# Keys and values of an encoder layer's input projection by pairs of k tiles, seven block products for 14 of 32 pairs

## The chip, the cores and the metric

The kernel runs on one core of one Trainium2 chip, in one launch. The metric is the device time in microseconds, as the median of several runs. Engines are named as in the profile: PE (matmuls; PEld is its weight load), DVE (the vector engine), ACT (the scalar engine), POOL (GpSimd) and SP, which only issues DMAs.

## What is computed

One encoder layer on 256 tokens with 2048 features, all in float32: a layer norm, an input projection to six groups of 1024 columns, two kinds of attention, an output projection, and a gated feed-forward network. Cut to what matters here:

```python
h = layer_norm(x, ln_in_g, ln_in_b)                      # x: (256, 2048)
proj = h @ w_in                                          # (2048, 6144)
na_q, na_k, na_v, d_q, d_k, d_v = split(proj, 6)         # 1024 columns each
na_out = neighbourhood_attention(na_q, na_k, na_v, na_rpb)          # 8 heads of 128
diff_out = rms_norm(differential_attention(d_q, d_k, d_v, lam, rel_bias_table), diff_subln_g)  # 4 heads
h = layer_norm(ALPHA * h + concat(na_out, diff_out) @ w_out, ln1_g, ln1_b)
h = layer_norm(ALPHA * h + (silu(h @ w_gate) * (h @ w_up)) @ w_down, ln2_g, ln2_b)
```

## The kernel before

**Matmuls.** Every float32 operand is cut into a rounded high part and the remainder, and a product is three matmuls: high by high, high by low, low by high. A *unit* is one k tile (128 rows) of one group's weights, 1024 columns wide. The six groups of the input projection are worked off in the order dq, dk, dv, nq, nk, nv, 16 units each; then come w_out (o0 and o1), the gate and up projections (f, g and u groups) and w_down. There are two token tiles, t = 0 and 1. In the input projection before the change, `mm_step` multiplies one unit by one token tile: six matmuls of 128x512, so 24 for a pair of units and both token tiles. The first eight units of dq (`NF0`) are multiplied for t = 0 in plain float32, unsplit, since nothing has been split yet ("whole" steps, two slow matmuls each).

**Pairs.** The gate, up and down projections already take their units in pairs (`add_group(..., seven)`). A pair is a 2x2 block matrix on each side. Plain pairs take eight block products; pairs named in `SEVEN` take seven (Winograd's form of Strassen's scheme). One block product is three matmuls. Seven products need sums of weight blocks and sums of token blocks ("forms", made by `more_forms`), each of which is split into high and low parts again. `seven_parts` lists this work for the weights of a pair: eleven operations on ACT and DVE in place of four. At the end of a group, `ffn_ends` combines the products on DVE into four blocks and hands each to `block_end`.

**Who sets the order.** The program is one stream per engine, written by a planner in the kernel: it keeps a clock for each engine, walks the list of PE steps (`steps`), and between them emits weight splits (`next_part`) up to `AHEAD_S` = 24 steps ahead and side work (attention heads, transposes, forms: `Side`), as its own clocks find it due. Engines then run their streams in order and wait for each other by semaphores. All SBUF tiles of 4 KB a partition come from one pool of 46 slots; a weight load needs a free slot, and SP issues loads in order.

**Names in rows.** `sl` is a slot, `acc` a PSUM bank, `nb`, `s` and `o` are small rings; `hT` is the transposed, split, normalised input; `h` are the normalised rows in their natural layout, which the residual sum of w_out needs again. Nearly every instruction is recorded at one helper line (L53, after the change L54), so groups are told apart by tiles and shapes.

Of the kernel before, what the change touches and what calls it, by code (L numbers as in the profile page):

```python
# [252 lines left out]
def layer_kernel(ctx: ExitStack, tc: tile.TileContext, A: dict, out: bass.AP):  # L253
# [61 lines left out]
    def chunk(ts, c):  # L315
        return ts[c // 2][:, (c % 2) * 512 : (c % 2) * 512 + 512]
# [47 lines left out]

    h_d = dram.tile([2 * P, D], F32, name="h_d")
    mid_d = dram.tile([NFC * P, 1024], F32, name="mid_d")
# [54 lines left out]
    def mm_step(t, u):  # L421
# [14 lines left out]
        if t == 1:  # L436
            leave(hi, lo)
            g, k = un["group"], un["k"]
            if k % 4 == 3:
                if g == "nv":  # L440
                    leave(*hT_tiles[k // 4])
                elif g == ("o", 1):
                    leave(*mixT_tiles[k // 4])
# [18 lines left out]
    L2 = 8  # L462
    R0 = 3
    R1 = 8
# [61 lines left out]
    def ln_side(key, t, g, b, store, tiles, n_whole):  # L526
# [10 lines left out]
        for c in range(4):  # L537
            while (key, t, c, "norm") not in have:
                yield None
            if t == 1 and c % 2:  # L540
                leave(g[c // 2], b[c // 2])
            yield "pe", [chunk(h[t], c)]
            if c not in tiles:
                new_T(store, tiles, c)
            bk = pe_transpose4(chunk(h[t], c))
            if key == "1":
                nc.gpsimd.dma_start(h_d[t * P : (t + 1) * P, c * 512 : (c + 1) * 512], chunk(h[t], c))
                if c % 2:
                    leave(h[t][c // 2])
                if c not in hF:  # L550
                    hF[c] = slot([P, 4, S])
                f = hF[c][:, :, t * P : (t + 1) * P]
                nc.scalar.copy(f, bk.rearrange("p (a b) -> p a b", b=P))
                have["hF", c] = have.get(("hF", c), 0) + 1
                if t == 0 and 4 * c < n_whole:
                    for i in range(4):
                        whole[key][4 * c + i] = f[:, i, :]
                    have[key, "whole", c] = 1
                side.add(part_split(key, t, c, f, tiles[c], t == 0 and 4 * c < n_whole))
                if t == 1:  # L560
                    for i in range(2):
                        side.add(more_forms(2 * c + i))
            elif t == 0 and 4 * c < n_whole:
                f = ring("nb", 2, (P, 4, P))
                nc.scalar.copy(f, bk.rearrange("p (a b) -> p a b", b=P))
# [3 lines left out]
                side.add(whole_split(key, c, f, tiles[c]))  # L569
            else:  # L570
                evac_T(bk, *tiles[c], t)
                have[key, t, c] = 1

    def whole_split(key, c, f, parts):
        return part_split(key, 0, c, f, parts, True)

    def part_split(key, t, c, f, parts, late):
# [7 lines left out]
        have[key, t, c] = 1  # L585
        if key == "1":
            used(("hF", c), 4, hF[c])

    hF, forms, halves, form_slots = {}, {}, [], []

    def more_forms(i):
        c, k = i // 2, 2 * (i % 2)
        while have.get(("hF", c), 0) < 2:
            yield None
        yield "dve", [hF[c]]
        ab, cd = hF[c][:, k : k + 2, :P], hF[c][:, k : k + 2, P:]
        if i in SEVEN:  # L600
            n = 4
            f = ring("s", 4, (P, 4, P))
# [534 lines left out]
    def products(u):  # L1137
# [7 lines left out]
        def f(m):  # L1145
            return lambda: forms[u if is_down(u) else i][m]

# [47 lines left out]
    def take_product(u, n):  # L1195
# [11 lines left out]
        if over:  # L1207
# [3 lines left out]
            if u == SE - 2:  # L1211
                leave(*[x for c in range(4) for x in h1T_tiles[c]], *form_slots)
            if is_down(u):
# [85 lines left out]

    ln1 = {}  # L1300

    ln2 = {}

# [6 lines left out]
    def group_out(t, name, a):  # L1310
        if name in ("dq", "dk", "nq", "nk"):
# [3 lines left out]
            nc.vector.tensor_scalar(nat[:, 512:], a[1], sc, None, op0=ALU.mult)  # L1315
            side.add(qk_side(name, t, nat), first=True)
            if t == 1 and name == "dk":
                for hd in range(DF_H):
                    side.add(diff_head(hd))
            if t == 1 and name == "nq":  # L1320
                for hd in range(NA_H):
                    side.add(na_head(hd))
        elif name in ("dv", "nv"):
# [71 lines left out]
    def steps():  # L1395
# [74 lines left out]
    class Step:  # L1470
# [18 lines left out]
        def possible(self):  # L1489
            if self.kind == "product":  # L1490
                k = units[self.u]["k"]
                if is_down(self.u):
# [122 lines left out]
```

## Time and profile before

| | us |
|---|---|
| median of 3 runs (1127.6 to 1128.8) | 1128.45 |
| the profiled execution's own time | 1128.12 |
| its span, first to last instruction | 1126.0 |
| PE busy in the span | 1110.7 |
| DVE busy | 929.1 |
| ACT busy | 596.9 |

The profiled execution is 2.1 us longer than its span and 0.3 us below the median of the runs. PE is busy nearly throughout, and the granted clock is 0.998 of full speed. The input projection runs from about 29 us to about 320 us of the span, the last attention heads until about 333 us; DVE is busy two thirds of that stretch and nearly all of the feed-forward network.

### The profile page before, as it was taken

What the parts mean: (1) busy time and instruction counts of PE and PEld (TensorE: products, weight loads), DVE (VectorE), ACT (ScalarE), POOL (GpSimd) and SP (SyncE); (2) the same over time, 40 slices, a digit from 0 to 9 for tenths busy, and PEclk for the clock granted to TensorE, in tenths of its full rate; (3) what the DMA queues carried; (4) which work ended last, traced back from release to release, by engine and by line L of the source; (5) the groups of instructions that cost most, each with busy time, mean ns of one, the idle gap of its engine ahead of it and who ended that gap; (6) DMA issues with size and microseconds to landing.
All of it is one profiled execution on the core that took longest, in us unless ns stands there. A gap on an engine that the chain in (4) does not pass through costs nothing.

```text
span 1126.0 us, 14140 instructions
## 1 busy us (share of the span) xinstructions
PE 1110.7 (99%) x5028; PEld 903.8 (80%) x5028; DVE 929.1 (83%) x1263; ACT 596.9 (53%) x781; POOL 59.6 (5%) x111
## 2 busy tenths in 40 slices
PE   8999999999999999999999999999999999999997
PEld 4788888888788876888888888888888888878885
DVE  7863876547773669999999999999999999799865
ACT  5552556434563228656556556566566566545630
POOL 2000003110100020000000000000000000000001
PEclk9999999999999999999999999999999999999999
DMA  9764548795766754655754755855756877667752
GB/s 332 246 204 156 166 146 172 177 206 187 162 218 231 243 183 135 210 197 173 268 206 164 278 205 164 282 190 178 271 208 223 289 265 281 217 223 281 251 164 75
DMA packets 70407, 237.15 MB, mean 211 GB/s; under 512 B 8516, under 2 KB 9924, under 8 KB 70336
## 3 DMA queue, kind: packets, MB, share of 16 engines
q1 hardware_dynamic: 65008, 220.49, 57.7%
q0 software_dynamic: 5168, 15.68, 6.8%
q8 instruction: 39, 0.64, 0.2%
q14 instruction: 32, 0.26, 0.1%
q10 hardware_dynamic: 160, 0.08, 0.0%
HBM read 226.25 MB, written 9.97 MB: 210 GB/s over the span
## 4 chain that ended last, share of the span: by engine, by line
PE 49%; issue 41%; DVE 5%; POOL 2%; ACT 2%; DMA 1%; POOLq 0%; DVEq 0%; ACTq 0%
PE acc L53 49%; DVE sl L53 3%; POOL mid_d L53 1%; ACT s L53 1%; DVE stats L53 1%; DVE s L53 1%; DMA mid_d<-nb 1%; ACT sl L53 1%; POOL rstd L53 0%; DMA nb<-in_ln_in_b_dram 0%; POOL h_d L53 0%; POOL rs L53 0%; ACT o L53 0%; DVE o L53 0%; ACT nb L53 0%
## 5 line engine op out<-in xcount | busy, mean ns | idle before, releaser
L53 PE MATMUL acc<-sl,sl 128*128 128x512 f32 (+1 forms) x4676 | 1062.8, 388 | 2.3 <-DVE sl L53 1.4
L53 PEld LDWEIGHTS acc<-sl,sl 128*128 128x128 f32 x4676 | 860.6, 188 | 183.7 <-issue 6.2
L53 DVE TENSOR_TENSOR sl<-sl,sl 128x1024 fp32r<-128x1024 f32 (+3 forms) x710 | 682.7, 1015 | 44.0 <-ACT sl L53 35.4
L53 ACT ACTIVATE sl<-sl 128x1024 fp32r<-128x1024 f32 (+1 forms) x530 | 498.6, 994 | 272.3 <-DVE sl L53 138.4
L53 ACT ACTIVATE sl<-acc 128x256 fp32r<-128x256 f32 (+2 forms) x70 | 33.2, 498 | 92.5 <-PE acc L53 74.0
L53 DVE TENSOR_TENSOR sl<-acc,sl 128x256 fp32r<-128x256 f32 (+2 forms) x94 | 54.8, 596 | 28.4 <-ACT sl L53 21.6
L53 DVE TENSOR_TENSOR sl<-sl 128x512 f32<-128x512 f32 (+1 forms) x76 | 41.2, 556 | 0.0
L53 DVE SCALAR_TENSOR_TENSOR sl<-sl,acc 128x512 f32<-128x512 f32 x10 | 6.8, 677 | 36.6 <-PE acc L53 36.6
L53 POOL DMA_DIRECT2D mid_d<-nb x22 | 11.9, 542 | 458.6 <-ACT nb L53 458.6
L53 ACT COPY sl<-acc 128x512 f32<-128x512 f32 x30 | 16.5, 587 | 34.9 <-PE acc L53 34.9
L53 DVE TENSOR_SCALAR sl<-acc 128x512 f32<-128x512 f32 x8 | 5.5, 688 | 34.2 <-PE acc L53 34.2
L53 ACT COPY nb<-acc 128x512 f32<-128x512 f32 x24 | 14.0, 585 | 34.9 <-PE acc L53 30.4
L53 ACT ACTIVATE s<-s 128x512 f32<-128x512 f32 x20 | 12.3, 632 | 22.8 <-DVE s L53 22.8
L53 POOL DMA_DIRECT2D nb<-in_na_rpb_dram x32 | 19.7, 624 | 85.7 <-DVE s L53 85.7
L53 ACT ACTIVATE s<-s,mx 128x256 f32<-128x256 f32 x32 | 15.9, 499 | 15.4 <-DVE mx L53 15.4
L53 PE MATMUL acc<-ident,s 128*128 128x128 f32 x136 | 20.5, 274 | 2.3 <-DVE s L53 1.7
L53 PEld LDWEIGHTS acc<-ident,s 128*128 128x128 f32 x136 | 16.5, 140 | 7.3 <-issue 1.9
L53 PEld LDWEIGHTS acc<-ident,sl 128*128 128x128 f32 x128 | 15.0, 140 | 7.3 <-issue 3.5
L53 DVE TENSOR_TENSOR sl<-sl,acc 128x512 f32<-128x512 f32 x16 | 10.6, 680 | 12.3 <-PE acc L53 12.2
L53 DVE SCALAR_TENSOR_TENSOR sl<-sl,rstd,sl 128x512 f32<-128x512 f32 x22 | 16.5, 752 | 4.0 <-POOL rstd L53 3.1
L53 DVE BATCH_NORM_STATS2 stats<-sl 128x6 f32<-128x512 f32 x24 | 16.3, 691 | 3.0 <-DMA sl<-in_x_dram 2.4
L53 PE MATMUL acc<-ident,sl 128*128 128x128 f32 x128 | 17.6, 273 | 0.5 <-DVE sl L53 0.4
(78 smaller groups left out, 224.4 us busy)
## 6 DMA issues: line engine op xcount, KB each, us to landing
sl<-in_w_in_dram SPq DMA_DIRECT2D x96, 512.0 KB, 4.8
sl<-in_w_down_dram SPq DMA_DIRECT2D x88, 512.0 KB, 6.0
sl<-in_w_gate_dram SPq DMA_DIRECT2D x80, 512.0 KB, 4.4
sl<-in_w_up_dram SPq DMA_DIRECT2D x80, 512.0 KB, 4.5
sl<-in_w_out_dram SPq DMA_DIRECT2D x32, 512.0 KB, 5.0
sl<-mid_d SPq DMA_DIRECT2D x14, 512.0 KB, 4.0
mid_d<-nb POOLq DMA_DIRECT2D x22, 256.0 KB, 3.3
sl<-in_w_gate_dram SPq DMA_DIRECT2D x16, 256.0 KB, 4.4
```

What stands on the lines that cost most here:

```text
L53: result = getattr(self.engine, op)(*args, **kw)
```

## The change

The groups dk, dv, nk and nv are now taken by pairs too. `SEVEN_IN` names the pairs with seven products: pairs 0, 2, 4 and 6 of dk and nk, pairs 0, 2 and 4 of dv and nv, 14 of 32 in all; the other 18 take eight products. dq and nq stay as they were.

- The normalised input now goes the way that the rows ahead of the feed-forward network went already: each chunk of transposed rows is copied to a slot (`hF`), split from there, and the forms are made from it, now under keys ("in" or "1"). Pair 6 needs both kinds of forms for "in".
- After its transposes each chunk of normalised rows is written to DRAM by POOL (`h_in`, eight DMAs of 256 KB), its slots are given back, and four loads of 512 KB on SP bring the rows back at unit 10 of o0.
- `R0` falls from 3 to 1: the second token tile of dq catches up with the first by the end of dq, because a pair needs both.
- The four groups end in `block_end`, which adds the products into a natural tile on DVE; keys are then transposed and values split (`v_side`) from there.
- Plain forms use ring `o` in place of half of ring `s`, in the feed-forward network too.

```diff
+SEVEN_IN = dict(dk=(0, 2, 4, 6), dv=(0, 2, 4), nk=(0, 2, 4, 6), nv=(0, 2, 4))
...
-        add_group(name, range(KT), [W_IN[:, off : off + 1024]], hT)
+        add_group(name, range(KT), [W_IN[:, off : off + 1024]], hT, SEVEN_IN.get(name))
...
-        if un["group"] == ("d", 0) and un["k"] == 24:
+        if (un["group"], un["k"]) in ((("o", 0), 10), (("d", 0), 24)):
+            key = "in" if un["group"][0] == "o" else "1"
             for t in range(2):
                 h[t] = [slot([P, 1024]) for _ in range(2)]
                 for i in range(2):
-                    nc.sync.dma_start(h[t][i], h_d[t * P : (t + 1) * P, i * 1024 : (i + 1) * 1024])
+                    nc.sync.dma_start(h[t][i], h_d[key][t * P : (t + 1) * P, i * 1024 : (i + 1) * 1024])
...
-    R0 = 3
+    R0 = 1
...
+            nc.gpsimd.dma_start(h_d[key][t * P : (t + 1) * P, c * 512 : (c + 1) * 512], chunk(h[t], c))
+            if c % 2:
+                leave(h[t][c // 2])
+            if (key, c) not in hF:
+                hF[key, c] = slot([P, 4, S])
+            f = hF[key, c][:, :, t * P : (t + 1) * P]
+            nc.scalar.copy(f, bk.rearrange("p (a b) -> p a b", b=P))
...
+            side.add(part_split(key, t, c, f, tiles[c], t == 0 and 4 * c < n_whole))
+            if t == 1:
+                for i in range(2):
+                    side.add(more_forms(key, 2 * c + i))
...
+        n, plain = 4 * ANY[key, i][0], 2 * ANY[key, i][1]
+        f = ring("s", 4, (P, 4, P)) if n else None
+        g = ring("o", 2, (P, 2, P)) if plain else None
...
+        if name in SEVEN_IN:
+            if (t, half) == (0, 0):
+                natural[name] = [slot([P, 1024]) for _ in range(2)]
+            nat = natural[name][t]
+            nc.vector.tensor_tensor(nat[:, half * 512 : half * 512 + 512], a, b, op=op)
+            have[name, "blocks"] = have.get((name, "blocks"), 0) + 1
+            if have[name, "blocks"] == 4:
+                for t in range(2):
+                    natural_out(name, t, natural[name][t])
...
+            if units[u]["pairs"]:
+                if u % 2 == 0:
+                    for n in range(len(products(u))):
+                        yield u, n
+                t1 = u + 1
+                continue
```

Counted over the built programs, PE has 42 matmuls of 128x512 fewer (three for each of 14 pairs) and else the same. DVE has 134 instructions more: 18 of 1024 columns, 90 net of 512, 10 net of 256 and 16 of 128. ACT has 39 more.

**The start of DVE's stream, before.** DVE has just normalised the second token tile's last chunk. `sl_284` and `sl_286` are the low parts of the weights of dq's units 8 and 0, `sl_308` those of unit 9; rows from `acc` are low parts of transposed input.

```order
L53 SCALAR_TENSOR_TENSOR sl_77<-sl_77,mv_215,sl_135 128x512
L53 SCALAR_TENSOR_TENSOR sl_77<-sl_77,rstd_217,sl_137 128x512
L53 TENSOR_TENSOR sl_199<-acc_269,sl_198 128x4x128
L53 TENSOR_TENSOR sl_284<-sl_211,sl_276 128x1024
L53 TENSOR_TENSOR sl_286<-sl_94,sl_263 128x1024
L53 TENSOR_TENSOR sl_221<-acc_290,sl_220 128x4x128
L53 TENSOR_TENSOR sl_230<-acc_297,sl_229 128x4x128
L53 TENSOR_TENSOR sl_308<-sl_242,sl_278 128x1024
```

**The same place in the change.** `sl_334`, `sl_360` and `sl_372` are now the low parts of units 8, 0 and 9 of dq; `s_285`, `s_305` and `o_291`, `o_362` are forms, `sl_290`, `sl_293` and `sl_310` their low parts.

```order
L54 TENSOR_TENSOR s_285<-sl_207 128x128 x2
L54 TENSOR_TENSOR s_285<-sl_207,s_285 128x128 x2
L54 TENSOR_TENSOR o_291<-sl_207 128x256
L54 TENSOR_TENSOR s_305<-sl_230 128x128 x2
L54 TENSOR_TENSOR s_305<-sl_230,s_305 128x128 x2
L54 TENSOR_TENSOR sl_200<-sl_207,sl_199 128x4x128
L54 TENSOR_TENSOR sl_290<-s_285,sl_290 128x512
L54 TENSOR_TENSOR sl_293<-o_291,sl_293 128x256
L54 TENSOR_TENSOR sl_334<-sl_213,sl_294 128x1024
L54 TENSOR_TENSOR sl_223<-sl_230,sl_222 128x4x128
L54 TENSOR_TENSOR sl_310<-s_305,sl_310 128x512
L54 TENSOR_TENSOR sl_360<-sl_95,sl_271 128x1024
```

Ahead of the low part of unit 8 there now stand the forms of two chunks and their low parts, and between units 8 and 0 another low part of a form, where there was nothing.

**PE at the first unit of dk, before.** `sl_490` and `sl_492`, named first, are the high and low parts of the unit's weights, `sl_198` and `sl_199` those of the input; the two accumulators are the unit's two halves of columns, for t = 0.

```order
L53 MATMUL acc_547<-sl_490,sl_198 128x512
L53 MATMUL acc_548<-sl_490,sl_198 128x512
L53 MATMUL acc_547<-sl_492,sl_198 128x512
L53 MATMUL acc_548<-sl_492,sl_198 128x512
L53 MATMUL acc_547<-sl_490,sl_199 128x512
L53 MATMUL acc_548<-sl_490,sl_199 128x512
```

**PE at the same place in the change.** One accumulator is one block product, three matmuls each; `sl_290` now are forms of the input, `sl_631` and `sl_632` sums of weight blocks, and the row with `ident` is a transpose of dq.

```order
L54 MATMUL acc_697<-sl_499,sl_199 128x512 x2
L54 MATMUL acc_697<-sl_499,sl_200 128x512
L54 MATMUL acc_701<-sl_508,sl_199 128x512
L54 MATMUL acc_701<-sl_634,sl_199 128x512
L54 MATMUL acc_701<-sl_508,sl_200 128x512
L54 MATMUL acc_707<-sl_508,sl_290 128x512
L54 MATMUL acc_707<-sl_634,sl_290 128x512
L54 MATMUL acc_707<-sl_508,sl_290 128x512
L54 MATMUL acc_712<-ident,sl_685 128x128 x4
L54 MATMUL acc_719<-sl_631,sl_290 128x512
L54 MATMUL acc_719<-sl_632,sl_290 128x512
L54 MATMUL acc_719<-sl_631,sl_290 128x512
```

What was one unit by one token tile has become products of a pair, with sums of blocks on both sides; side work stands between products.

**DVE in nv, before.** After the exponentials of heads of the neighbourhood attention, the rows that scale them, and then `sl_2420`, the low part of the weights of nv's unit 7, and `sl_2432`, that of unit 8.

```order
L53 RECIPROCAL sums_2355<-sums_2355 128x2
L53 TENSOR_SCALAR s_1938<-s_1938,sums_2355 128x256 x2
L53 RECIPROCAL sums_2367<-sums_2367 128x2
L53 TENSOR_SCALAR s_2044<-s_2044,sums_2367 128x256 x2
L53 RECIPROCAL sums_2384<-sums_2384 128x2
L53 TENSOR_SCALAR s_2088<-s_2088,sums_2384 128x256 x2
L53 TENSOR_TENSOR sl_2420<-sl_2233,sl_2407 128x1024
L53 TENSOR_TENSOR sl_2432<-sl_2272,sl_2430 128x1024
```

**DVE in nv, in the change.** The same kind of rows, and behind them `sl_2849`, the low part of nv's unit 13.

```order
L54 RECIPROCAL sums_2779<-sums_2779 128x2
L54 TENSOR_SCALAR s_2237<-s_2237,sums_2779 128x256 x2
L54 ISA s_2763,mx_2835<-acc_2827,s_2763 128x256
L54 ISA mx_2835 128x1
L54 ISA s_2763,mx_2835<-acc_2827,s_2763 128x256
L54 ISA mx_2835 128x1
L54 TENSOR_SCALAR mx_2835<-mx_2835 128x2
L54 RECIPROCAL sums_2805<-sums_2805 128x2
L54 TENSOR_SCALAR s_2303<-s_2303,sums_2805 128x256 x2
L54 TENSOR_TENSOR sl_2849<-sl_2748,sl_2847 128x1024
L54 RECIPROCAL sums_2817<-sums_2817 128x2
L54 TENSOR_SCALAR s_2718<-s_2718,sums_2817 128x256 x2
```

In both, weight splits stand behind rows that wait for ACT's exponentials: those of units 7 and 8 before, that of unit 13 now.

## Rows read from the trace of the kernel before

**Rows 1.** The page: busy us by engine; DVE in 40 slices, tenths

```profile
PE 1110.7 (99%) x5028; PEld 903.8 (80%) x5028; DVE 929.1 (83%) x1263; ACT 596.9 (53%) x781; POOL 59.6 (5%) x111
...
DVE  7863876547773669999999999999999999799865
```

**Rows 2.** Windows: length, busy us by engine, granted clock, DMA share, GB/s

```profile
0.00:28.00 28.00, 24.75 (x90) 13.21 (x91) 21.18 (x33) 15.71 (x26) 7.24 (x18) 1.00 0.94 332
...
28.00:336.00 308.00, 305.60 (x1490) 254.91 (x1489) 201.46 (x349) 154.35 (x260) 26.07 (x47) 1.00 0.67 184
...
476.00:504.00 28.00, 28.00 (x125) 23.19 (x124) 27.40 (x33) 13.41 (x17) 0.00 (x0) 1.00 0.62 216
```

**Rows 3.** Timeline of PE at the start: start us, duration, tiles, count

```profile
26.43 3.60 PE L53 MATMUL acc<-sl,nb 128*128 128x512 f32 x8
29.47 10.11 PE L53 MATMUL acc<-sl,sl 128*128 128x512 f32 x42
39.51 1.02 PE L53 MATMUL acc<-sl,rel 32*4 32x512 f32 x2
```

**Rows 4.** Timeline of DVE at the start

```profile
26.23 2.35 DVE L53 TENSOR_TENSOR sl<-sl,sl 128x1024 fp32r<-128x1024 f32 x2
...
31.43 1.28 DVE L53 TENSOR_TENSOR sl<-nb,sl 128x512 fp32r<-128x512 f32 x2
32.64 11.44 DVE L53 TENSOR_TENSOR sl<-sl,sl 128x1024 fp32r<-128x1024 f32 x10
43.99 0.67 DVE L53 COPY diag<-acc 4x512 f32<-4x512 f32 x1
```

**Rows 5.** Timeline of DVE where the feed-forward network's forms begin

```profile
420.66 1.28 DVE L53 TENSOR_TENSOR sl<-sl,sl 128x512 fp32r<-128x512 f32 x2
421.86 0.48 DVE L53 TENSOR_TENSOR s<-sl 128x128 f32<-128x128 f32 x2
422.27 0.61 DVE L53 TENSOR_TENSOR s<-sl,s 128x128 f32<-128x128 f32 x2
422.79 0.42 DVE L53 TENSOR_TENSOR s<-sl 128x256 f32<-128x256 f32 x1
423.13 0.68 DVE L53 TENSOR_TENSOR sl<-sl,sl 128x512 fp32r<-128x512 f32 x1
```

**Rows 6.** Timeline of PE there; in brackets idle time and its releaser

```profile
428.41 3.40 PE L53 MATMUL acc<-sl,sl 128*128 128x512 f32 x12 [0.57 <-DVE sl L53]
432.22 13.19 PE L53 MATMUL acc<-sl,sl 128*128 128x512 f32 x55 [0.41 <-DVE sl L53]
```

**Rows 7.** Waits of PE, 28 to 336 us: us in total, times, longest

```profile
PE acc L53 <- DVE s L53: 1.7, 2, 1.5
PE acc L53 <- DVE o L53: 0.6, 1, 0.6
```

**Rows 8.** Waits of DVE, 28 to 336 us: us in total, times, longest

```profile
DVE sl L53 <- ACT sl L53: 49.0, 51, 4.6
...
DVE o L53 <- POOL rs L53: 7.2, 4, 3.6
DVE s L53 <- DMA nb<-in_na_rpb_dram: 5.9, 2, 3.1
```

**Rows 9.** Groups of DVE, 28 to 336 us: busy, mean ns, idle before

```profile
L53 DVE TENSOR_TENSOR sl<-acc,sl 128x256 fp32r<-128x256 f32 x32 | 13.3, 421 | 10.2 <-ACT sl L53 10.2
...
L53 DVE SCALAR_TENSOR_TENSOR sl<-acc,subg,sl 128x256 fp32r<-128x256 f32 x8 | 3.8, 480 | 3.0 <-ACT sl L53 3.0
```

**Rows 10.** DMA issues, 160-180, 215-235, 235-255 us: count, KB, us to landing

```profile
sl<-in_w_in_dram SPq DMA_DIRECT2D x7, 512.0 KB, 3.9
...
sl<-in_w_in_dram SPq DMA_DIRECT2D x8, 512.0 KB, 14.0
nb<-in_na_rpb_dram POOLq DMA_DIRECT2D x12, 64.0 KB, 9.6
...
sl<-in_w_in_dram SPq DMA_DIRECT2D x5, 512.0 KB, 14.5
```

More of the change, by code (lines that the diff above doesn't have):

```diff
@@ L363, in layer_kernel @@
     raw, wh, wl = {}, {}, {}
-    h_d = dram.tile([2 * P, D], F32, name="h_d")
+    h_d = {key: dram.tile([2 * P, D], F32, name=f"h_{key}") for key in ("in", "1")}
     mid_d = dram.tile([NFC * P, 1024], F32, name="mid_d")
@@ L439, in mm_step @@
             if k % 4 == 3:
-                if g == "nv":
-                    leave(*hT_tiles[k // 4])
-                elif g == ("o", 1):
+                if g == ("o", 1):
                     leave(*mixT_tiles[k // 4])
@@ L545, in ln_side @@
             bk = pe_transpose4(chunk(h[t], c))
[L546 to L565, printed above, removed]
+            nc.gpsimd.dma_start(h_d[key][t * P : (t + 1) * P, c * 512 : (c + 1) * 512], chunk(h[t], c))
[5 more added lines that the diff above has]
+            nc.scalar.copy(f, bk.rearrange("p (a b) -> p a b", b=P))
+            have["hF", key, c] = have.get(("hF", key, c), 0) + 1
+            if t == 0 and 4 * c < n_whole:
                 for i in range(4):
@@ L1145, in f @@
         def f(m):
-            return lambda: forms[u if is_down(u) else i][m]
+            key = "in" if u < FFN else "1"
+            return lambda: (forms[u] if is_down(u) else forms[key, i, 0 if units[u]["seven"] else 1])[m]
         def b(row, col):
@@ L1211, in take_product @@
             if u == SE - 2:
-                leave(*[x for c in range(4) for x in h1T_tiles[c]], *form_slots)
+                leave(*[x for c in range(4) for x in h1T_tiles[c]], *form_slots["1"])
+            if name == "nv" and units[u]["k"] == KT - 2:
+                leave(*[x for c in range(4) for x in hT_tiles[c]], *form_slots["in"])
             if is_down(u):
@@ L1298, in block_end, with natural_out, v_side @@
             side.add(mid_side(2 * name[1] + half, t, m))
-    ln1 = {}
-    ln2 = {}
+    ln1, ln2, natural = {}, {}, {}
+    def natural_out(name, t, nat):
+        if name[1] == "v":
+            side.add(v_side(name, t, nat), first=True)
+            return
+        side.add(qk_side(name, t, nat), first=True)
+        if t == 1 and name == "dk":
+            for hd in range(DF_H):
+                side.add(diff_head(hd))
+        if t == 1 and name == "nq":
+            for hd in range(NA_H):
+                side.add(na_head(hd))
+    def v_side(name, t, nat):
+        hi, lo = vt[name, t] = (slot([P, 1024], F32R), slot([P, 1024], F32R))
+        yield "act", [nat]
+        nc.scalar.activation(hi, nat, AF.Copy)
+        yield "dve", [hi]
+        nc.vector.tensor_tensor(lo, nat, hi.bitcast(F32), op=ALU.subtract)
+        leave(nat)
+        have[name] = have.get(name, 0) + 1
     def group_end(t, name):
@@ L1315, in group_out @@
             nc.vector.tensor_scalar(nat[:, 512:], a[1], sc, None, op0=ALU.mult)
[L1316 to L1322, printed above, removed]
+            natural_out(name, t, nat)
         elif name in ("dv", "nv"):
@@ L1400, in steps @@
         for u in range(SG):
+            if units[u]["pairs"]:
[3 more added lines that the diff above has]
+                t1 = u + 1
+                continue
             f = u < NF0 or FFN <= u < FFN + NF1
@@ L1404, in steps @@
                 continue
-            if u < FFN - 40:
+            if units[u]["last"] and u + 1 < FFN and units[u + 1]["pairs"]:
+                behind = 0
+            elif u < FFN - 40:
                 behind = max(1, NF0 - (u - NF0) // R0)
@@ L1496, in possible @@
                     )
-                return ("forms", k // 2) in have and all(("1", t, k // 4) in have for t in range(2))
+                key = "in" if self.u < FFN else "1"
+                return ("forms", key, k // 2) in have and all((key, t, k // 4) in have for t in range(2))
             return possible(self.t, self.u, self.f)
```

71 lines of the change are left out of this document (32 added, 39 removed).

## The prediction

> **What bounds the kernel now.** I read the page first. PE is busy 1110.7 of 1126.0 us, and DVE's slices lie between 3 and 8 tenths in the first third and at 9 from there on [rows 1]. A busy PE is no proof of a PE at its pace, so I took the pace from windows. [...] There, from 28 to 336 us, PE is busy 305.60 of 308 us but DVE only 201.46, with the clock at 1.00 [rows 2]. So PE bounds the stretch and DVE has 106 us to spare. The list of waits shows what PE loses in it: 1.7 and 0.6 us, all for attention rows on DVE [rows 7]. In its first 28 us PE is busy 24.75 [rows 2].
>
> **What is removed.** 42 matmuls: three for each of 14 pairs, and PE's stream is otherwise the same in count. 42 x 0.224 = 9.4 us off the engine that bounds.
>
> **What is added on DVE.** From the change's counts and start-to-start times of back-to-back rows: ten splits of 1024 columns take 43.99 - 32.64 = 11.35 us, 1.135 each; two of 512 take 32.64 - 31.43 = 1.21, 0.605 each [rows 4]; four form operations of 128 columns take 422.79 - 421.86 = 0.93, 0.23 each, and one of 256 0.34 [rows 5]. 18 x 1.135 + 90 x 0.605 + 10 x 0.34 + 16 x 0.23 = 20.4 + 54.5 + 3.4 + 3.7 = 82 us. DVE then needs 201.5 + 82 = 283.5 us where the stretch offers 308 - 9.4 = 298.6: 95%, under the 97.9% that cost PE nothing. On average it is hidden behind PE; without that cover it would cost all of the 82. ACT's 39 added operations lie in a stretch where it is busy 154.35 of 308 us [rows 2] and are costed at nothing.
>
> **The start, where it isn't hidden.** DVE begins the split for dq's unit 8 at 26.23 us, the first thing it does after the norm [rows 4]. PE's eight float32 units end at 26.43 + 3.60 = 30.0 us, and it wants that split then [rows 3]. So there are 2.6 us of margin after the split's 1.135. In the change DVE comes to the same point with the same work done, since it exchanges one low part for idle time, but ahead of unit 8 now stand two sets of four form operations, one of 256 columns, and three low parts of 512, 512 and 256: 0.93 + 0.34 + 0.93 + 0.60 + 0.60 + 0.34 = 3.7 us. Unit 8 is ready at 26.2 + 3.7 + 1.1 = 31.1, which is 1.1 us late. From there PE takes one step of six matmuls every 1.34 us and DVE owes one split of 1.135 a step, so it gains 0.2 us a step but has more forms to pay: 1.2 us of low parts before unit 0, 0.34 before unit 9, 0.6 before unit 1, 0.93 before unit 2, 0.94 before unit 11. Summed down the stream: unit 2, due at 35.4, comes at 38.7; unit 11, due at 40.75, at 44.2. The lateness never passes 3.5 us, and what PE has waited by then it doesn't wait again. I take 3.5 us. Bounds: the same forms ahead of the feed-forward network cost PE 0.57 + 0.41 = 1.0 us [rows 6], which is the lower end; there DVE had from 420.66 to 428.41, 7.8 us, before PE wanted a split, here 3.8, and the 4.0 us that are missing make the upper end 5.0.
>
> **Behind the start.** DVE catches up in the second half of dq, where the second token tile meets splits that are already there. The eight writes of normalised rows stand on POOL; only the first lies ahead of the second tile's reciprocal root, and weights landing early in that stretch hide 2 MB of traffic. The reload stands on SP ahead of w_out's loads and is wanted only when o0 ends. Both at nothing. If that cover went, the 2.1 MB would cost 6 us at the 332 GB/s of the first window [rows 2].
>
> **nk and nv.** A seven-product pair asks DVE for three splits of 1024 and five of 512, 6.4 us, against 21 matmuls, 4.7; a plain one for 2.3 against 5.4. In nv the eight heads come on top. Walking down DVE's order there, a split of unit 13 behind four softmaxes comes about 1 us late, and the pair of units 2 and 3 about 0.7. The kernel before pays 2.3 us for such things [rows 7]; I take half as much again, +1.2. Bounds: if heads meet PE better than now, -1.7; if weights come late as in the second rival, +5.0.
>
> **Sum.** -9.4 + 3.5 + 1.2 = -4.7 us. On the profiled execution, 1128.1 us with a span of 1126.0, that is 1123.4 with a span of 1121.3; it lies 0.3 us below the median of 1128.45, so the median becomes 1123.8. From that stretch on the order is nearly as before, and I take nothing from it. With all bounds: -9.4 + 1.0 - 1.7 = -10.1 to -9.4 + 5.0 + 5.0 = +0.6, so 1118.3 to 1129.0.
>
> **Rival: the whole gain.** Most of the start's forms fit into gaps, and heads cost no more than now: -9.4 + 1.0 = -8.4, 1120.0 us, and 1118.3 with the lower bound in nv. For it: the feed-forward network pays just that. Against it: the 2.6 us of margin are a row, the 3.7 us are a row's durations.
>
> **Rival: weights come late.** Slots are the scarce thing: input parts, forms, both attentions and pairs share 46. In the change's order, the slot into which nk's unit 8 is loaded is last read 19.1 us of matmul work ahead of its first use; before it was 33.8. And the neighbourhood bias is loaded in nk, in rows of 256 bytes: at 160-180 us weights land in 3.9 us, beside bias loads in 14.0 and 14.5 [rows 10]. 14.2 us of landing and some 5 of splits (two rounds through ACT and DVE) make 19.2 against 19.1. With loads seven units ahead, that paces a unit at 19.2 / 7 = 2.74 us where PE asks 180 x 0.224 / 16 = 2.52: 16 x 0.22 = 3.5 us in nk, and about 1.5 for nv's unit 13, whose slot is free only 14.4 us ahead. -9.4 + 3.5 + 5.0 = -0.9, 1127.5 us, which counts as no change. Against it: with the same landing of 14 us before, PE waited for nothing in this stretch but attention rows [rows 7]. [...]
>
> **Rival: DVE becomes the bound, and the kernel slower.** DVE's idle time from 28 to 336 us is not all free. It waits 49.0 us for ACT, 7.2 for POOL and 5.9 for bias loads [rows 8], and of the waits for ACT 10.2 and 3.0 us belong to heads, a low part right behind its high part [rows 9]. If these 26.3 us remain whatever stands ahead of them, DVE needs 283.5 + 26.3 = 309.8 of 298.6 us: 11.2 late, and -9.4 + 3.5 + 11.2 = +5.3, 1133.8 us. It decides once more than 15.1 + 5.9 = 21 us of waits stay (the spare time, and the gain left after the start). Against it: when DVE runs late, ACT's part is done before DVE asks, and the wait shrinks by itself, as in the feed-forward network's 97.9%.
>
> **From cases to numbers.** A difference under 0.2%, 2.3 us, can't be told from no change here. The forecast (1120.8 to 1126.0) gets 0.56, the whole gain 0.14, late weights 0.19 and DVE as the bound 0.11. Of late weights 0.02 fall below 1126.2. Faster: 0.56 + 0.14 + 0.02 = 0.72; same 0.17; slower 0.11. To leave out no more than 2 in 10 the range cuts the far part of the gain and all of the slower case: 1118.8 to 1128.2.
>
> **What would show it.** Right: 42 matmuls fewer; PE idle by 3 to 4 us between 30 and 45 us, released by DVE `sl`; DVE at 9 tenths in the slices of dk, dv, nk and nv; waits of PE in nv of 2 to 4 us for DVE; the feed-forward network's windows as before, only earlier. Wrong: no idle time at 30 to 45 us (the whole gain), waits of PE in nk behind ACT or DVE that themselves wait for weights (late weights), or PE losing over 5 us in dv or nv with DVE busy throughout (DVE as the bound). A granted clock under 1.00 after the new stall would break every term; the windows before show 1.00 [rows 2].

## The result and the profile after

The changed kernel takes 1138.4 us (median of four runs, 1137.0 to 1140.3) against 1128.1: a ratio of 1.0092, with a 95% interval of 1.0074 to 1.011. It is 0.9% slower, clear of the interval, where I had forecast 1123.8 and a range up to 1128.2. The profiled execution took 1140.3 us with a span of 1138.4; it is the slowest of the four, at a mean granted clock of 0.994, and the fastest, 1137.0 us, had 0.997. Of its page, the busy times and the clock in 40 slices:

```profile
PE 1110.3 (98%) x4986; PEld 899.2 (79%) x4986; DVE 1010.0 (89%) x1397; ACT 625.9 (55%) x820; POOL 65.5 (6%) x119
...
PEclk9999999998999999999999999999999999999999
```

PE has 42 matmuls fewer than in [rows 1] and is as busy as before, so the matmuls that are left took longer; its idle time in the span rose from 15.3 to 28.1 us. DVE has 81 us more, as worked out (82). In the tenth slice the clock shows a dip; no slice of the kernel before has one. Windows (length, busy us by engine, granted clock, DMA share, GB/s), the first two also in [rows 2]:

```profile
28.00:336.00 308.00, 295.72 (x1396) 240.95 (x1395) 272.30 (x464) 176.28 (x285) 30.02 (x53) 0.99 0.64 188
476.00:504.00 28.00, 28.00 (x125) 23.17 (x125) 27.89 (x32) 15.81 (x18) 0.00 (x0) 1.00 0.54 179
...
256.00:263.00 7.00, 5.12 (x23) 3.86 (x21) 4.33 (x8) 4.22 (x5) 0.00 (x0) 1.00 0.34 137
264.00:270.00 6.00, 5.41 (x17) 4.46 (x18) 5.89 (x9) 0.71 (x2) 0.00 (x0) 0.50 0.65 194
```

The feed-forward regime is what it was, 125 matmuls per window. The input projection lost: PE is idle 12.3 of 308 us, where it was 2.4. The two short windows are the dip: between 264 and 270 us TensorE was granted 0.50 of its full clock. What it did before it fell stands in PE's timeline (start, duration; in brackets idle time and releaser):

```profile
257.78 3.35 PE L54 MATMUL acc<-sl,sl 128*128 128x512 f32 x14
264.59 1.09 PE L54 MATMUL acc<-ident,sl 128*128 128x128 f32 x4 [3.47 <-DVE sl L54]
265.33 4.19 PE L54 MATMUL acc<-sl,sl 128*128 128x512 f32 x9
```

PE stood still for 3.5 us at the entry of nv, three matmuls behind the last one on nk's weights, and then nine matmuls took 4.19 us, 0.47 each. PE waited for DVE; DVE's timeline just ahead says for what DVE waited:

```profile
235.42 3.49 DVE L54 TENSOR_TENSOR sl<-sl,sl 128x1024 fp32r<-128x1024 f32 x3
242.73 0.69 DVE L54 TENSOR_TENSOR sl<-sl 128x512 f32<-128x512 f32 x1 [3.83 <-DMA sl<-in_w_in_dram]
...
252.02 3.50 DVE L54 TENSOR_TENSOR sl<-sl,sl 128x1024 fp32r<-128x1024 f32 x3 [2.64 <-ACT sl L54]
...
258.72 2.62 DVE L54 TENSOR_TENSOR sl<-sl,sl 128x512 f32<-128x512 f32 x4 [2.60 <-DMA sl<-in_w_in_dram]
```

It waited for weights, and for ACT, which had itself waited for a load:

```profile
249.98 2.96 ACT L54 ACTIVATE sl<-sl 128x1024 fp32r<-128x1024 f32 x3 [4.09 <-DMA sl<-in_w_in_dram]
```

Counted along SP's order of loads, these are the weights of nk's units 12 to 14 and of nv's unit 1; their loads took 13.7 to 20.7 us to land. That is the rival "weights come late". Its stall stands at nv's first pair, not where the rival had it (nk's unit 8 and nv's unit 13).

It isn't the whole of the loss, though. **A table by stage** shows the rest, and it judges every run below. For each PE instruction I took the time from its start to the next one's start, less the median of that for its shape (0.227 us for 128x512), and summed what is left: the time that PE lost to waits and to a low clock. A stage ends with the last matmul on its group's weights; its entry is its first few matmuls. DVE is its busy time from 72 to 318 us. Stages are of the profiled execution, the time is the median. Sums in the text are of figures before rounding.

| | start, dq | dk | dv | nq | nk | nv | o0 | rest | DVE | time |
|---|---|---|---|---|---|---|---|---|---|---|
| before | 9.1 | 0.0 | 0.2 | 1.2 | 0.0 | 2.6 | 0.0 | 16.1 | 155.7 | 1128.1 |
| after | 12.2 | 0.1 | 2.3 | 2.4 | 1.5 | 8.8 | 2.8 | 21.5 | 212.0 | 1138.4 |
| e1 | 12.0 | 0.1 | 2.3 | 2.6 | 1.1 | 2.0 | 2.8 | 18.0 | 218.5 | 1129.9 |
| e2 | 9.4 | 0.0 | 0.1 | 1.1 | 0.0 | 2.6 | 0.0 | 16.8 | 155.8 | 1128.8 |
| e3 | 12.3 | 0.0 | 0.2 | 1.1 | 7.9 | 9.7 | 4.6 | 21.1 | 177.7 | 1151.0 |
| e4 | 12.3 | 0.1 | 2.2 | 2.6 | 0.0 | 2.6 | 0.0 | 20.4 | 188.2 | 1134.0 |
| e5 | 10.1 | 3.8 | 2.1 | 2.7 | 1.1 | 2.0 | 2.9 | 17.0 | 217.8 | 1130.4 |
| e6 | 12.5 | 0.1 | 1.9 | 5.6 | 0.0 | 9.2 | 5.9 | 16.6 | 213.3 | 1140.5 |
| e7 | 9.8 | 0.0 | 0.1 | 1.2 | 0.0 | 2.6 | 0.0 | 18.6 | 155.9 | 1131.7 |
| e8 | 12.3 | 0.1 | 2.2 | 2.4 | 1.1 | 2.7 | 0.0 | 16.5 | 209.1 | 1129.8 |
| e9 | 12.2 | 0.1 | 0.8 | 3.3 | 0.0 | 11.0 | 1.9 | 17.9 | 216.7 | 1136.0 |
| e10 | 12.1 | 0.1 | 3.7 | 3.6 | 0.7 | 4.5 | 4.1 | 20.2 | 211.9 | 1138.0 |
| e11 | 12.3 | 0.1 | 3.6 | 3.6 | 0.0 | 0.9 | 3.3 | 16.3 | 218.1 | 1130.8 |
| e12 | 10.9 | 1.4 | 3.8 | 3.6 | 0.0 | 0.9 | 3.2 | 16.2 | 218.3 | 1129.2 |
| e13 | 8.6 | 0.0 | 2.6 | 3.4 | 0.0 | 3.2 | 0.0 | 16.6 | 205.9 | 1134.9 |
| e14 | 12.5 | 1.7 | 8.9 | 2.4 | 3.8 | 7.1 | 2.8 | 16.8 | 223.9 | 1145.2 |
| e15 | 9.9 | 0.0 | 0.1 | 1.1 | 0.0 | 3.2 | 0.0 | 18.0 | 178.2 | 1127.7 |
| e16 | 9.8 | 0.0 | 0.8 | 2.5 | 0.6 | 2.3 | 0.0 | 18.6 | 195.0 | 1127.9 |
| e17 | 10.7 | 0.7 | 0.2 | 1.2 | 0.0 | 3.2 | 0.0 | 16.9 | 193.7 | 1127.3 |
| e18 | 10.6 | 0.7 | 0.2 | 1.2 | 7.7 | 8.9 | 0.0 | 20.3 | 187.6 | 1142.5 |

After against before: 9.5 us less in matmuls; 3.1 lost at the start, 14.0 from dk to o0, 5.4 behind: 13.0 in all, where the spans differ by 12.4.

### The profile page after: what moved, and what is told of

Read it like the earlier page. It is cut to its first block, busy times and chain, and to the rows that moved or that the text cites. A ratio compares the mean times of both kernels' runs of the same rounds, so it can differ in the third digit from the quotient of the medians.

```text
span 1138.4 us, 14289 instructions
## 1 busy us (share of the span) xinstructions
PE 1110.3 (98%) x4986; PEld 899.2 (79%) x4986; DVE 1010.0 (89%) x1397; ACT 625.9 (55%) x820; POOL 65.5 (6%) x119
## 4 chain that ended last, share of the span: by engine, by line
PE 42%; issue 41%; DVE 8%; DMA 6%; POOL 1%; ACT 1%; POOLq 0%; SPq 0%; DVEq 0%; ACTq 0%
PE acc L54 42%; DVE sl L54 7%; DMA sl<-in_w_in_dram 4%; DVE s L54 1%; POOL mid_d L54 1%; ACT sl L54 1%; DMA mid_d<-nb 1%; DVE stats L54 1%; DMA sl<-in_w_out_dram 0%; POOL h L54 0%; POOL rstd L54 0%; DMA sl<-in_x_dram 0%; DVE mx L54 0%; POOLq L1637 0%; DVE mv L54 0%
## 5 line engine op out<-in xcount | busy, mean ns | idle before, releaser
L54 PE MATMUL acc<-sl,sl 128*128 128x512 f32 (+1 forms) x4666 | 1078.0, 391 | 10.5 <-DVE sl L54 8.4
L54 PEld LDWEIGHTS acc<-sl,sl 128*128 128x128 f32 x4666 | 860.4, 189 | 200.9 <-DVE sl L54 16.9
L54 DVE TENSOR_TENSOR sl<-sl,sl 128x1024 fp32r<-128x1024 f32 (+3 forms) x792 | 744.9, 994 | 30.6 <-ACT sl L54 18.6
L54 ACT ACTIVATE sl<-sl 128x1024 fp32r<-128x1024 f32 (+1 forms) x570 | 528.3, 981 | 287.3 <-DVE sl L54 141.4
L54 DVE TENSOR_TENSOR sl<-acc,sl 128x512 f32<-128x512 f32 (+2 forms) x108 | 64.0, 608 | 15.4 <-ACT sl L54 8.4
L54 DVE TENSOR_TENSOR sl<-sl 128x512 f32<-128x512 f32 (+1 forms) x90 | 50.9, 577 | 4.1 <-DMA sl<-in_w_in_dram 3.8
L54 ACT ACTIVATE sl<-acc 128x256 fp32r<-128x256 f32 (+2 forms) x52 | 23.6, 463 | 50.5 <-PE acc L54 30.2
L54 ACT COPY sl<-acc 128x512 f32<-128x512 f32 x42 | 23.3, 587 | 39.3 <-PE acc L54 39.3
L54 ACT ACTIVATE s<-s 128x512 f32<-128x512 f32 x20 | 12.3, 632 | 24.7 <-DVE s L54 24.7
L54 PE MATMUL acc<-ident,s 128*128 128x128 f32 x136 | 20.7, 275 | 2.8 <-ACT nb L54 2.7
L54 PEld LDWEIGHTS acc<-ident,s 128*128 128x128 f32 x136 | 16.8, 140 | 7.8 <-ACT nb L54 3.1
L54 DVE TENSOR_TENSOR sl<-sl,acc 128x512 f32<-128x512 f32 x16 | 10.6, 681 | 13.5 <-PE acc L54 13.4
L54 DVE SCALAR_TENSOR_TENSOR sl<-sl,rstd,sl 128x512 f32<-128x512 f32 x22 | 16.5, 752 | 4.6 <-POOL rstd L54 3.8
L54 DVE BATCH_NORM_STATS2 stats<-sl 128x6 f32<-128x512 f32 x24 | 16.3, 691 | 3.0 <-DMA sl<-in_x_dram 2.5
L54 DVE SCALAR_TENSOR_TENSOR sl<-sl,mv,sl 128x512 f32<-128x512 f32 x24 | 17.8, 747 | 0.3 <-ACT sl L54 0.2
```

Of the source, the lines that this page charges most:

```text
L54: result = getattr(self.engine, op)(*args, **kw)
```

## The experiments

**Bias loads alone (e1, e2).** The neighbourhood bias is a window that slides by one float per partition, so four rows of it lie within one run of 157 floats:

```diff
-                nb[...].rearrange("p (a b) -> p a b", b=GW),
-                bass.AP(..., ap=[[1, GW], [31, 4], [1, GW]]),
+                nb[..., : 3 * 31 + GW],
+                bass.AP(..., ap=[[1, GW], [1, 3 * 31 + GW]]),
```

> The changed kernel with every instruction where it stood; only the 32 bias loads of the neighbourhood heads change: per partition one run of 157 floats (628 bytes) in place of four runs of 64 (256 bytes), and the bias is read out of it on DVE by strides of 31. Late weights (bias loads hold w_in back in nk): landings of w_in in nk fall from 13 to 20 us to under 8, the 3.6 us stall of PE at the end of nk, the half clock behind it and most of nk's 1.5 us go: 8 to 9 us less, about 1130, and the granted clock stays at 1.00 through nk and nv. DVE's own order as the cause: the stall stays, 1138 within 1 us.

> The kernel before with the same 32 loads as in e1 and else every instruction where it stood: the control. PE waited for no weight there, so both theories expect 1128.1 within 0.5 us, though w_in in nk lands in under 8 us instead of 14.

1129.9 and 1128.8 us. DMA from 217 to 262 us, after (queue and kind, packets, MB, share of 16 engines; then issues, KB each, median us to landing):

```profile
q1 hardware_dynamic: 2015, 7.34, 48.4%
q0 software_dynamic: 512, 1.05, 37.3%
...
sl<-in_w_in_dram SPq DMA_DIRECT2D x14, 512.0 KB, 13.3
nb<-in_na_rpb_dram POOLq DMA_DIRECT2D x16, 64.0 KB, 10.5
```

And e1, the same stretch:

```profile
q1 hardware_dynamic: 2296, 8.37, 55.4%
q0 software_dynamic: 512, 0.64, 10.5%
...
sl<-in_w_in_dram SPq DMA_DIRECT2D x16, 512.0 KB, 4.7
nb<-in_na_rpb_dram POOLq DMA_DIRECT2D x16, 39.2 KB, 5.9
```

One seventh as many bytes as the weights' took 37.3% of the engines' time; in runs of 628 bytes 10.5%, and weights land in 4.7 us instead of 13.3. Per MB that is 36% of the engines in runs of 256 bytes and 16% in runs of 628. The stall at the entry of nv is gone, and so is the half clock that came with it (from 256 to 278 us e1 has PE busy 21.96 of 22 us at a granted clock of 1.00): the median falls by 8.5 us, and in the profiled executions PE loses 7.2 us less from dk to o0. The control didn't move. Late weights are shown as a cause, and the bias loads as what makes them late. But e1 still isn't faster than the kernel before: from dk to o0 it loses 6.9 us more, and PE's waits from 28 to 336 us in e1 are all for DVE:

```profile
PE acc L54 <- DVE sl L54: 6.6, 8, 1.7
PE acc L54 <- DVE o L54: 1.4, 1, 1.4
```

**By place (e3, e4).** `SEVEN_IN` names only two of the four groups.

> Only nk and nv by pairs (21 matmuls saved in place of 42), dk and dv as before the change; forms are still made at the start. Late weights: the start's 3.1 us and the losses in nk and nv stay, the 2.2 us at the entry of dv go: 1138.4 + 4.7 - 2.2 = about 1141, clock down again at the end of nk. DVE as the cause (heads and pairs in one group): the same losses in nv and o0, but nothing lost before nv: about 1139 with the clock at 1.00 in nk.

> Only dk and dv by pairs (21 matmuls saved), nk and nv as before the change. Late weights: a plain unit needs its weights later and its splits take two steps, so the loss in nk, nv and o0 (12.6 us over before) goes for the most part: 1138.4 + 4.7 - 10 = about 1133, or less where the later clock drops stay away. DVE as the cause: likewise, since DVE has room again in nk and nv, but w_in landing in 15 us in nk then does no harm either way. Start and dv entry cost 3.1 + 2.2 against 4.7 saved: no gain over 1128.1 is expected.

1151.0 and 1134.0. e4 came as late weights expect: with plain units in nk and nv no more is lost there than before the change. e3 is a miss: 10 to 12 us above what either theory said, lost in nk, nv and o0, while dv lost nothing. In nk w_in lands in 17.6 us in the median, and ACT's waits from 217 to 276 us are mostly for it:

```profile
ACT sl L54 <- DMA sl<-in_w_in_dram: 22.0, 9, 5.5
```

Neither forecast had a term for the clock: from 259 to 338 us the trace of e3 has four stretches at 0.50, 3.4 us each, and by the table's measure PE loses 6.2 us in them.

**More lead, own bias loads (e9, e10).**

```diff
-            while ... self.kind != "product" or room() > KEPT + 2):
+            while ... self.kind != "product" or room() > (3 if self.u < FFN else KEPT + 2)):
```

> The changed kernel with its own bias loads, and only the rule changed by which weights of the input projection's pairs are loaded: further than 3 units ahead when more than 3 slots are free, in place of more than 8. Late weights are a matter of lead as much as of slow landings: with loads up to 8 units ahead nk gets its weights in time though they land in 13 to 20 us, most of the stall at the end of nk and its half clock go, 1131 to 1134. Rival: slots are what is scarce, loads can't come earlier or take slots from splits, and the time stays at 1138 within 1.5 us or rises.

> The changed kernel with its own bias loads; in the input projection loads go further ahead when more than 5 slots are free in place of 8, and splits that are not near leave 3 slots free in place of 6. If splits that come at the last moment cause what e1 still loses at the entries of dv and nk and in o0 (2.1, 1.1 and 2.8 us), these fall to about half, -3 us, and the weights in nk come earlier as in e9: about 1130. If the adding up at a group's end causes it, only the part of e9 is seen.

1136.0 and 1138.0. In e9 the weights land as slowly as in the changed kernel (12.4 us in the median from 217 to 262 us), but with loads that start earlier PE waits for nothing there and nk loses nothing: lead cures late weights. nv loses 11.0 in place of 8.8, and of ACT's and DVE's waits there only 1.8 us are for weights. That the slots which the loads take are then missing for splits, as the rival has it, is not shown. e10 came out 8 us above its forecast of 1130.

**Start, first pairs, parking, nv (e5 to e8).** e5 makes a form wait for a unit of dq:

```diff
-        while have.get(("hF", key, c), 0) < 2:
+        while have.get(("hF", key, c), 0) < 2 or (key == "in" and have.get("t1", -1) < HELD + i):
             yield None
```

> e1 (1129.9) with the forms of the input held back: form i is not made before the second token tile of dq has reached unit 4 + i, so that the splits of dq's units 8, 0, 9, 1 and so on stand first on DVE again; dk and all behind it in e1's order. If the start's loss (12.0 us over the matmuls' own time in e1, 9.1 before) is the forms' place on DVE, it falls to about 9.5 and the time by 2.5 us, to 1127.4. Rival: it is the early catching up of the second token tile (R0), which stays: 1129.9 within 0.7 us.

> e1 with seven products for pairs 1, 3, 5 (and 6 of the keys) in place of 0, 2, 4 (and 6): the same 42 matmuls fewer, but the first pair of each group is a plain one, which asks 2.3 us of DVE in place of 6.4 just when the group before is added up there. If that meeting is what PE waits for at the entry of dv (2.1 us), nk (1.1) and in nv (2.0), some 3 us go: about 1127. Rival: the adding up alone (5 us of DVE) holds the next group back whichever pair comes first: 1129.9 within 0.7 us.

> No pairs in the input projection, no forms, none of the 42 matmuls saved and the bias loads as in the kernel before; what stays of the change is the copy of the transposed rows to a slot, the rows parked in DRAM and read back, and the second token tile catching up by the end of dq. The prediction took all of that at nothing: 1128.3 within 0.7 us. Rival: the traffic of 4 MB or the reload on SP costs up to 6 us: 1130 to 1134.

> e1 without pairs in nv (9 matmuls more, +2.0 us). If the 2.8 us that PE loses in o0's first units are DVE behind with nv's pairs, their adding up and eight heads together, they go, and nv loses about what it did before (2.6 in place of 2.0): 1129.9 + 2.0 - 2.8 + 0.6 = 1129.7. Rival: the heads alone cause it, the 2.8 us stay and the time rises to about 1132.

1130.4, 1140.5, 1131.7, 1129.8. e5: the start fell from 12.0 to 10.1, so the forms' place accounts for 1.9 of the 2.9 us that e1 lost there; but DVE now makes them when dk wants its first splits. PE's timeline of e5 shows the loss there, and a window behind it nine matmuls at a granted clock of 0.50:

```profile
69.95 0.94 PE L55 MATMUL acc<-sl,sl 128*128 128x512 f32 x3
72.70 3.54 PE L55 MATMUL acc<-sl,sl 128*128 128x512 f32 x10 [1.80 <-DVE sl L55]
```

```profile
74.10:77.30 3.20, 3.20 (x9) 2.46 (x8) 3.17 (x4) 1.56 (x2) 0.00 (x0) 0.50 0.06 23
```

e6 is a plain miss: nk lost nothing, but nq, nv and o0 13 us more than in e1, 5.8 of them in stretches at half clock. e7 came out as its rival had it: the rows that are parked in DRAM and read back, with the early second token tile, cost 0.7 us at the start and nothing in the rest of the input projection; behind it something does (below). e8: without pairs in nv the 2.8 us in o0 go, for 2.0 us of matmuls: in nv pairs pay nothing.

**Splits made earlier (e11, e12).** Both have e1's loads; splits that are not near leave 3 slots free, not 6, and e12 sets `URGENT = 4`.

> e10 with the bias loads in runs of 628 bytes as in e1 (1129.9). Splits made at the last moment as the cause of what is left: 1129.9 - 3 to 5 = 1125 to 1127, faster than the kernel before. The adding up on DVE as the cause: 1129.9 within 1 us.

> e11 and splits for the next four steps in place of three put ahead of side work such as forms. The start loses 12.0 us in e1 and 9.1 in the kernel before; here the forms should take up less of DVE just there, about 10.5: 1 to 2 us less than e11. Rival, from e5: what the start gains comes back at the entry of dk, and the time is e11's.

1130.8 and 1129.2. dv's and nk's entries are free, and heads (attention work) in dv and nq wait instead: from dk to o0 e11 loses 11.3 us and e12 12.9, in place of e1's 10.8. e5, e11 and e12 had moved e1's loss and none had shrunk it: was it DVE's load?

**DVE's load by itself (e13, e14).** e13 in the kernel before, e14 on e1:

```diff
+        if KT <= u < 6 * KT:
+            n = slice(0, 640)
+            nc.vector.tensor_tensor(wl[u][:, n], raw[u][:, n], wh[u][:, n].bitcast(F32), op=ALU.subtract)
...
-            nc.vector.tensor_tensor(s["lo"], s["t"], ...)
+            nc.gpsimd.tensor_tensor(s["lo"], s["t"], ...)
```

> The kernel before, nothing paired, with DVE work alone added: each low part of the 80 units from dk to nv is formed a second time in its first 640 columns, the same values again, about 0.74 us each, 59 us in all (the change adds 56 us from 72 to 318 us). DVE's load as the cause of what e1 still loses from dv to o0 (6.9 us over the kernel before): PE waits some 5 us more there, about 1133. What is particular to pairs as the cause (adding up at a group's end, splits in six to eleven steps that must all stand before the first product, slots): 1128.3 within 1 us, since single splits can be made well ahead.

> e1 (1129.9) with every instruction where it stood, but the 28 low parts of 1024 columns of the summed blocks of the 14 seven-product pairs are formed on POOL in place of DVE: 28 x 1.135 = 32 us less on DVE, and POOL was idle there. DVE's load as the cause: the losses at the entries of dv and nk and in o0 (2.1, 1.1, 2.8 us) fall by half or more, 1126 to 1127. Rival: POOL takes several us for one of these, products 3 to 6 wait for it, or DVE slows while POOL works: 1132 or more.

1134.9 and 1145.2. In e13 nothing is paired; what is added is a second pass over 640 columns right behind each low part, for which PE then waits too. The added group of DVE, 68 to 318 us (busy, mean ns, idle before):

```profile
L53 DVE TENSOR_TENSOR sl<-sl,sl 128x640 fp32r<-128x640 f32 x73 | 60.2, 825 | 2.5
```

PE then loses 5.3 us more than in the kernel before, 4.6 of them in dv and nq, in waits for attention rows and splits (PE's waits, 112 to 318 us):

```profile
PE acc L53 <- DVE o L53: 2.8, 1, 2.8
PE acc L53 <- DVE sl L53: 1.9, 2, 1.6
PE acc L53 <- DVE s L53: 1.1, 2, 0.6
```

e14 was to take load away and added some: a low part takes 2935 ns on POOL, and DVE's own splits became slower beside it, 1670 ns against 1217 in e1 (groups from 68 to 318 us, POOL's of the whole span; the last row is e1's):

```profile
L54 POOL TENSOR_TENSOR sl<-sl,sl 128x1024 fp32r<-128x1024 f32 x28 | 81.8, 2935 | 85.6 <-ACT sl L54 82.0 <-PE acc L54 3.6
L54 DVE TENSOR_TENSOR sl<-sl,sl 128x1024 fp32r<-128x1024 f32 x65 | 106.3, 1670 | 1.9 <-ACT sl L54 1.9
```

```profile
L54 DVE TENSOR_TENSOR sl<-sl,sl 128x1024 fp32r<-128x1024 f32 x94 | 110.2, 1217 | 1.5 <-ACT sl L54 1.4
```

The slowing goes with the overlap: of e14's rows, the 43 that overlap no such operation of POOL take 1216 ns on average, as in e1, and the seven that lie wholly inside one take 2995. So e14 tells nothing of a lighter DVE.

**Pairs only where DVE has room (e15 to e18).** All on e1's loads but e18.

```diff
-SEVEN_IN = dict(dk=(0, 2, 4, 6), dv=(0, 2, 4), nk=(0, 2, 4, 6), nv=(0, 2, 4))
+SEVEN_IN = dict(dk=(0, 2, 4, 6), nk=(0, 2, 4, 6))
```

> Only nk by pairs, with the bias loads of e1, forms of the input held back until the second token tile of dq has reached unit 8 + i, and R0 at 3 as in the kernel before: 12 matmuls fewer, 2.7 us. nk is a group with room on DVE (24.9 of 45 us busy in the kernel before) and no start to pay. DVE's load where it has no room as the cause: the start costs 9.1 us again, dv, nq and o0 lose what they lost before, nk's entry about 1: 1128.3 - 2.7 + 1 = 1126.6. If pairs cost what they save wherever they stand: 1128.3 within 0.7 us.

> e15 with dv by pairs too: 21 matmuls fewer, 4.7 us. In dv the differential heads already keep DVE busy 40 of 52 us in the kernel before, so 17 us more leave it nothing. DVE's load as the cause: dv and nq lose 3 to 4 us more than before, as in e13, and the 2.0 us that these 9 matmuls save are gone: e15's time or 1 us above it. Otherwise 2.0 us below e15.

> dk and nk by pairs (the two groups in which DVE has room: 18.3 of 40 and 24.9 of 45 us busy in the kernel before), 24 matmuls fewer, 5.4 us, bias loads of e1, splits for four steps ahead before side work as in e12. dk's forms must be made in dq: the start costs 1.5 to 3 us, dk's entry 1, nk's entry 1, the rest as before: 1128.3 - 5.4 + 4.5 = about 1127.4.

> e17 (1127.3) with every instruction where it stood and the bias loads as in the kernel before, in runs of 256 bytes. Late weights: w_in lands in nk in 12 us or more again, PE loses 3 to 8 us in nk and behind it. The parked rows: with them and 256-byte bias loads the 19th of the writes of the gate's product on POOL came 2.1 us after its data in the six kernels profiled, with either alone 0.3; it should come 2.1 us late here and cost PE about 1 us more in the feed-forward network. Together 1131 to 1136. If the choice of groups alone made e17 what it is: 1127.3 within 0.7 us.

1127.7, 1127.9, 1127.3, 1142.5. e17 is the one version below the kernel before: 0.9984, interval 0.9975 to 0.9992, 1.1 us; e15 and e16 can't be told from it, nor from the kernel before. In e16 the pairs of dv save 2.0 us, lose 2.7 in dv, nq and nk and win 0.9 in nv: nothing, as expected. e15's forecast was 1 us too low: nk's entry cost nothing, but the start 0.8 and nv 0.6 more; the 3.4 us at half clock in its feed-forward network are of the profiled execution, 1129.4 us, and don't explain the median. e18 has e17's instructions in e17's order and differs by the bias loads' bytes per run; it is 15.1 us slower, 6 above the upper end of its forecast. Weights land in 9.7 us there, not in 12 or more, and DVE stands behind the bias itself, with the splits behind it in its stream (issues from 217 to 262 us; DVE's waits from 217 to 300 us):

```profile
sl<-in_w_in_dram SPq DMA_DIRECT2D x15, 512.0 KB, 9.7
...
DVE s L54 <- DMA nb<-in_na_rpb_dram: 10.7, 4, 4.4
```

In the trace of e18 two stretches of 6.8 us and two of 3.4 are at 0.50; by the table's measure PE loses 7.6 us in them.

## Why the prediction was wrong

**Right:** 42 matmuls fewer by 0.224 us, which is 28.00 us over the 125 matmuls of the last window in [rows 2] (9.5 us by the table's 0.227); DVE's 82 us (80.9); the size of the start's +3.5 (3.1). Of the start only 1.3 us are idle time of PE between 30 and 45 us, where 3 to 4 were named as the sign; the rest lies in longer steps from one matmul to the next. e5 puts 1.9 us of the start down to the forms' place, and e7 0.7 to what stays of the change without forms.

**The step that failed is the cover, "On average it is hidden behind PE", and with it the term "nk and nv", +1.2 us with bounds of -1.7 and +5.0.** From dk to o0 PE lost 14.0 us more than before: 7.7 in nk and nv, past the upper bound, and 6.3 in dv, nq and o0, for which there was no term. Two causes share the 14.0.

*Late weights*, 7.2 us (the changed kernel less e1). The rival had the mechanism, the groups and the landing (14.2; 13.3 in the median now), and a price of 5.0. Its place was off: it had 3.5 us in nk as a steady pace and 1.5 at nv's unit 13, but nk lost 1.5 in all, of which 1.1 stay in e1, and the stall of 3.5 us stood at nv's first pair. With that stall came 6.8 us at a granted clock of 0.50, from 263.6 us, 1.0 us before the stall ended; PE lost 2.8 us more in them, and for that there was no term: I had named the danger for the start, and it came in nv. What failed is the rival's chance of 0.19. The argument against it, that PE waited for nothing with the same landing before, held for a slot lead of 33.8 us; the prediction's own walk gave the change 19.1 and 14.4, and e9 shows that more lead cures nk: 0.0 us lost there in place of 1.5, with a landing of 12.4.

*DVE's load*, 6.9 us (e1 less the kernel before). I took 95% of 298.6 us as hidden by the feed-forward network's 97.9% (27.40 of 28.00 us on DVE, with no idle time on PE [rows 2]), but no attention heads stand on DVE there. From 72 to 318 us they do: with 155.7 us of 246 busy (63%) PE loses 3.9 us from dk to o0, with 193.7 (79%) 5.3 in e17, with 205.9 (84%) 9.2 in e13, with 218.5 (89%) 10.8 in e1. e13 shows that added load alone makes heads and splits late in dv and nq, by 4.6 us, where e1 loses 3.5 more than before. In nk and o0 e13 loses nothing: that e1's 1.1 us in nk and 2.8 in o0 are of the same kind is argued and not shown; e8 ties those in o0 to nv's pairs. Load isn't all of it either: e6 has less (87%) and loses 22.6 us, by another choice of pairs and the order that follows from it. The rival "DVE becomes the bound" named 11.2 us; its form was another, not DVE busy throughout, but a split, an adding up or a head that stands behind another, 1 to 2 us at a time.

**"From that stretch on ... I take nothing" was wrong by 5.4 us** in the profiled execution. Of these, 2.1 follow from **the writes on POOL "at nothing"**, and 3.1 are lost in two stretches of 3.4 us at half clock, from 898.5 and from 1017.9 us; the first begins 0.3 us after the stall that the late write causes has ended. POOL's timeline before, and after; the column is the start, in brackets idle time and what ended it:

```profile
880.36 0.54 POOL L53 DMA_DIRECT2D mid_d<-nb  x1 [70.48 <-ACT nb L53]
883.57 0.54 POOL L53 DMA_DIRECT2D mid_d<-nb  x1 [2.67 <-ACT nb L53]
```

```profile
889.82 0.55 POOL L54 DMA_DIRECT2D mid_d<-nb  x1 [72.32 <-issue]
891.21 0.54 POOL L54 DMA_DIRECT2D mid_d<-nb  x1 [0.84 <-ACT nb L54]
```

Before, this write follows ACT's copy by 0.29 us; after, the first row shown by 2.13, and it waits for nothing that the profile shows. ACT's next copy waits for a write of that ring to land, 6.65 us in place of 4.50, and PE for that copy, 2.67 in place of 0.52. PE's timeline before, and after, and windows of the two stretches after:

```profile
888.42 0.66 PE L53 MATMUL acc<-ident,s 128*128 128x128 f32 x4 [0.52 <-ACT nb L53]
```

```profile
898.20 0.89 PE L54 MATMUL acc<-ident,s 128*128 128x128 f32 x4 [2.67 <-ACT nb L54]
...
899.00:901.50 2.50, 2.50 (x8) 1.92 (x8) 2.46 (x4) 2.50 (x4) 0.17 (x1) 0.50 0.54 215
1018.00:1021.00 3.00, 3.00 (x8) 2.34 (x7) 3.00 (x4) 1.93 (x3) 0.00 (x0) 0.50 0.90 309
```

The late write is there in all seven profiled kernels with parked rows and 256-byte bias loads together, e18 by forecast, and in none of the 13 others. Why the two add up to it was not found. In five of the seven a stretch at half clock begins within 1.5 us of the stall's end; in e7 and e9 none does. e7 is 3.2 us slower than before, mostly by this and the start.

**Open:** why the clock falls behind some stalls and not behind others (1.80 us at the entry of dk in e5: yes; 1.81 us at the entry of dv in the changed kernel: no); and why e9 loses more in nv, and e6 more than e1.

## What to carry to other kernels

A transfer of small runs is judged by what it does to the loads beside it: here weights landed in 13.3 us beside 1.05 MB of bias loads in runs of 256 bytes, and in 4.7 beside 0.64 MB in runs of 628 (e1). That stayed hidden in the kernel before, with a lead of 33.8 us by the prediction's walk; in the change, with 19.1 and 14.4, it cost 7.2 us. An engine's spare time is an average; where chains of side work share it, cost what is added by the group in which it falls: here a load of 84% already cost 5.3 us (e13). And put a price on the clock behind a stall that a change may bring: here 2.8 us on top of one of 3.5.

## What the runs showed of the hardware

POOL's work and DVE's were not independent in e14: beside 28 tensor_tensor operations of 1024 columns on POOL, 2.9 us each, DVE's of the same shape took 37% longer on average (1670 ns against 1217 in e1), and 3.0 us in place of 1.2 where they lay wholly inside one of POOL's. Some stalls of TensorE went with stretches at a granted clock of 0.50: 3.5 us with 6.8 us of it (2.8 us lost) and 2.7 us with 3.4 (1.5 lost) in the changed kernel, 1.8 us with 3.4 in e5. A stall of 1.8 us at another place of the changed kernel and those of 2.3 us in e7 and e9 did not. And in seven kernels one DMA on POOL was issued 2.1 us after its data were there, at the same place each time.
